# Two of four attention gate tiles computed as a seven-product pair in the last phase, not as filler in attention

## The chip, the core and the metric

The kernel runs on one core of a Trainium2 chip. The metric is the device time of one execution in microseconds; a kernel's time is the median of its timed runs. Beside them one execution was recorded by the hardware profiler, and every statement on what an engine did comes from that record.

## The reference

One layer of a decoder trunk, run in fp32 for 1024 prompt tokens and 64 sample tokens (8 sequences of 8) that share the weights. Cut to what matters here:

```
h = rmsnorm(x) * (1 + scale) + shift                  # width 1024
z = h @ w_in + b_in                                   # width 8456
a_u, a_v, a_g, b_q, b_k, b_v, b_g, c_qk, c_v, c_i, c_f, c_o, c_g, m_g = split(z)
ya = chunk_gmlp(a_u, a_v) * silu(a_g)
yb = sliding_window_attention(b_q, b_k, b_v) * silu(b_g)      # 8 heads of 64, window 128
yc = mlstm(c_qk, c_v, c_i, c_f, c_o) * silu(c_g)
merged = sum over the three branches of sigmoid(m_g[n]) * (y_n @ w_branch_n)
x_out = x + gate * (merged @ w_out)
```

The change concerns `b_g`, the 512 columns 2304 to 2816 of `w_in`: four channel tiles of 128, for all 1088 tokens, each put through `silu`.

## The kernel before

Every fp32 operand is split into a high and a low part (`hh`, `hl` for `h`), and a product is three matmuls: high by high, high by low, low by high. A channel tile against all tokens is worked in three chunks of 384, 384 and 320 tokens (`CH`), each of 8 k tiles x 3 matmuls.

The program runs in stages: the start, the mLSTM branch, the attention stage (pool `bph`), and the last phase. In the attention stage the order on TensorE is the order of the code (a manual schedule); the other engines' orders are set by the scheduler. A loop over steps `i` drives a pipeline of 16 prompt blocks (`Prompt(g, n)`: two key groups, eight blocks of 128 queries; here called blocks 0 to 15) and then 4 sample blocks. In step `i` the plan runs, in this order, `v` of block i-5 (the product with the values), `s` of block i-2 (the logits), `p` of block i-4 (the transposes of the probabilities), and `q` of block i (the transposes of the queries). After `s`, `p` and `q` a call of `filler` lets TensorE work on projections that attention does not wait for, so that VectorE and ScalarE have time for the softmax. A call ends at the first k tile at which the filled columns reach its share of `FILL`:

```
FILL = (11000, 11000)
PLAN = ((6, "y", 0), (5, "v", 0), (2, "s", 0.3), (4, "p", 0.3), (0, "q", 0.4))
order += [("a", s, n) for s in range(2) for n in range(9)]
order += [("b", f, ci) for f in range(4) for ci in range(3)][:-1]
```

The filler's order is: the query tiles (`q`, 256 columns for each 128 tokens), the gMLP rows (`a`, alike), and last the gates (`b`), tile `f` and chunk `ci`. A gate chunk's evacuation (`ev_b` in `bg_chunk`) is two ScalarE passes and one on VectorE, then a DMA from GpSimd's queue to the DRAM buffer `dsg`. The last chunk stays in PSUM across the end of the stage. Weights for the filler come in slabs of 256 columns, split by ScalarE and VectorE (L127, L128) into one of two `hl` buffers.

Between, VectorE also makes the sums `TT` of token halves and k halves for the last phase (`t_next`, L855 to L857 and L844).

A prompt block's softmax after the logits (L88 `pk<-KT,QT`): ScalarE copies and VectorE masks them (L1102, L1103), VectorE takes the maximum (L1106 to L1108, L1114), ScalarE the exponentials with their sums (L1111, L1115), VectorE adds the sink and takes the reciprocal (L1116, L1117), ScalarE scales (L1119); TensorE transposes (L92 `pu<-ident,Sm`); VectorE masks into `Pp` and `Pc` (L1131, L1134).

The last phase is a list `items` of TensorE pieces, each with weights prepared five items ahead (`LEAD`). Function `seven` forms two channel tiles as a pair: with channels, token halves and k halves as two by two blocks, seven products of 4 k tiles by 544 tokens replace eight. Each product is 4 x 3 matmuls on 288 tokens and as many on 256 (`CUT`); VectorE and ScalarE combine weights beforehand (`comb`, `w_split`, L1432, L1437, L1438) and results afterwards (`collect`), and `final` gets the four quarters. It is used for the gMLP's pairs and for the twelve pairs of merge gates (`gate_pair`). `gate_b(f, b)`, which stands behind the first branch's projections, multiplies a tile and token half of the attention result `dy` with the gates from `dsg`.

Of the kernel before, what the change touches and what calls it, by code (L numbers as in the profile page):

```python
# [11 lines left out]
AF = mybir.ActivationFunctionType  # L12
ALU = mybir.AluOpType
# [6 lines left out]
EPS = 1e-6  # L20
XP = 1115
XC = 1112
FILL = (11000, 11000)
PLAN = ((6, "y", 0), (5, "v", 0), (2, "s", 0.3), (4, "p", 0.3), (0, "q", 0.4))


# [3 lines left out]
CUT = ((0, 288), (288, 256))  # L30
# [11 lines left out]
def trunk_kernel(ctx: ExitStack, tc: tile.TileContext, I, O):  # L42
    nc = tc.nc
    V, S, G, T = nc.vector, nc.scalar, nc.gpsimd, nc.tensor

    w_in = I["w_in"][0]
# [30 lines left out]
    def slot(tag, shape, dt=F32, name=None):  # L77
        return sp.tile(shape, dt, tag=tag, name=name or tag)

    def ct(shape, name, dt=F32):  # L80
        return cp.tile(shape, dt, name=name)
# [13 lines left out]
    def kv(ap):  # L95
        return ap.rearrange("(k p) c -> p k c", p=128)

    def full(w, c0, n):
        v = kv(w[:, c0:c0 + n])
        return [v[:, 0:4], v[:, 4:8]]  # L100

    def pair(c0, c1):
# [3 lines left out]
    specs += [pair(2816 + 128 * h, 3328 + 128 * h) for h in range(1, 4)]  # L106
    specs += [pair(4360 + 128 * h, 4872 + 128 * h) for h in range(4)]
    specs += [full(w_in, 2048, 256), full(w_in, 1536, 256), full(w_in, 1792, 256),
              full(w_in, 512, 256), full(w_in, 768, 256), full(w_in, 2304, 256), full(w_in, 2560, 256)]

    slabs = {}

# [35 lines left out]
    cols = ct([128, 100], "cols")  # L148
    cwcol = ct([128, 32], "cwcol")
    bh = ct([128, 100], "bh")  # L150
    CAU, CAG, CBG, CQK, CO, CG, CM, CADA, CNG, CCB, CHN, CVN = 0, 4, 8, 12, 20, 24, 28, 52, 76, 84, 92, 96
# [323 lines left out]
    dsg = dp.tile([4, 128, NT], F32, name="dsg")  # L475
# [4 lines left out]
    with tc.tile_pool(name="cph", bufs=1, side="right", reuse_waits="tile") as c1:  # L480
# [303 lines left out]
        for h in range(1, 4):  # L784
            hl = next_slab()
            for s in range(2):
                f = 4 * s + h
# [89 lines left out]
    with tc.tile_pool(name="bph", bufs=1, side="right", reuse_waits="tile") as b1:  # L877
# [485 lines left out]
        def fill_steps():  # L1363
            order = [("q", 0, n) for n in range(9)]
            order += [("q", 1, n) for n in range(9)]
            order += [("a", s, n) for s in range(2) for n in range(9)]
            order += [("b", f, ci) for f in range(4) for ci in range(3)][:-1]
            for kind, a, c in order:
                yield from {"q": q_tile, "b": bg_chunk, "a": av_tile}[kind](a, c)
                done.add((kind, a, c))  # L1370

        fill = fill_steps()

        def filler(cols, until=None):
# [11 lines left out]
        for i in range(len(steps) + 6):  # L1386
            w = FILL[0] if i < 18 else FILL[1]
            for d, ph, share in PLAN:
# [15 lines left out]
    one.close()  # L1404


    w2r, w3, e2, w2 = (ctx.enter_context(tc.tile_pool(name=n, bufs=1, reuse_waits="tile")) for n in ("w2r", "w3", "e2", "w2"))
    banks = [0]

    def bank():  # L1410
# [3 lines left out]
    def part_(h, j):  # L1414
        return slice(HT * h + CUT[j][0], HT * h + CUT[j][0] + CUT[j][1])
# [4 lines left out]
    def mp(n, name):  # L1420
        return e2.tile([128, CUT[0][1]], F32, tag="mp", bufs=3, name=name)[:, :n]
# [39 lines left out]
    items = []  # L1461
# [134 lines left out]
    Q7 = (1, 6, 7, 5, 3, 2, 4)  # L1596
# [71 lines left out]
    def y_load(n):  # L1668
# [5 lines left out]
        for b in range(2):  # L1674
            c = slice(HT * b, HT * b + HT)
            for f in range(4):
# [2 lines left out]
                S.copy(yh[f][:, c], x)  # L1679
                V.tensor_tensor(yl[f][:, c], x, yh[f][:, c].bitcast(F32), ALU.subtract)  # L1680

    mh, ml = [None] * 8, [None] * 8
    lastm = [None] * 3

# [43 lines left out]
    def gate_rows(g):  # L1728
        def prep():
            for q in range(4):  # L1730
                if q % 2 == 0:
                    gst["t"] = gst.get("t", []) + [y2[0].tile([128, 2, 512], F32, tag=f"yh{2 + q // 2}", name="graw")]
                raw = gst["t"][-1][:, q % 2]
                with tc.issue_after(newest[0]):
                    nc.sync.dma_start(raw.rearrange("p (k c) -> p k c", k=2),
                                      kv(ada_w[:, 2048 + 256 * g:2304 + 256 * g])[:, 2 * q:2 * q + 2])
                gst[g, q] = raw

        def run(_):
            pm = gst[g] = bank()  # L1740
            for q in range(4):
                for kk in range(2):
                    i = 2 * (q % 2) + kk
                    mm(pm[32 * i:32 * i + 32, 0:256], sT[:, 2 * q + kk], gst[g, q][:, 256 * kk:256 * kk + 256], q < 2, q >= 2)
            gst[g, "s"] = mp(256, "gsb")
            S.copy(gst[g, "s"], pm[:, 0:256])
            gst[g, "m"] = mp(256, "mrow")[:9]
            nc.sync.dma_start(gst[g, "m"], ada_b[:, 2048 + 256 * g:2304 + 256 * g].broadcast_to([9, 256]))

        def run2(_):  # L1750
            pm, m = gst[g], gst[g, "m"]
            mm(pm[0:9, 256:512], sel, gst[g, "s"], True, True)
            V.tensor_tensor(m, m, pm[:9, 256:512], ALU.add)
            V.tensor_scalar(m, m, 0.5, None, ALU.mult)
            nc.sync.dma_start(drow[:, 256 * g:256 * g + 256], m)

        return [(prep, run), (None, run2)]
# [16 lines left out]
    gr = [x for g in range(4) for x in gate_rows(g)]  # L1774
    items += [(None, last_gate)] + it[0][:2] + [behind(t_late, 0, 1)] + it[0][2:4] + [behind(t_late, 2, 2), act(t_in_place, *((k,) for k in range(4)))] + it[0][4:5] + [act(t_late, (3,))] + it[0][5:]
    rest = it[1][:2] + [None] + it[1][2:3] + [None] + it[1][3:4] + [None] + it[1][4:5] + [None] + it[2][:1] + [None]
    rest += it[1][5:6] + [None] + it[1][6:] + [None] + it[2][1:2] + [None] + it[2][2:] + it[3]
    items += [x or gr.pop(0) for x in rest]

    def gate_b(f, b):  # L1780
        if not stage:
# [40 lines left out]
    for i, f in enumerate((0, 4, 1, 5, 2, 6)):  # L1822
        m_tiles(f)
        x = slot(("y0", "y1", "m2", "m3", "y4", "y5")[i], [128, NT], name="mgr")
# [19 lines left out]
    for i in range(4):  # L1844
# [4 lines left out]
        for n in tuple(range(9)) if i < 3 else (8,) + tuple(range(8)):  # L1849
# [15 lines left out]
            if n == 8:  # L1865
                t = mp(256, "ts")
# [39 lines left out]
```

## Time and profile before

| | |
|---|---|
| timed runs | 1182.39, 1181.17, 1179.51 us; median 1181.17 us |
| profiled execution | 1181.08 us, of which the core's span is 1179.4 us |
| mean granted TensorE clock | 0.996 |
| attention's prompt logits, first to last start | 404.3 to 526.9 us |
| gate finals in attention, first to last start (L1234) | 515.8 to 573.4 us |
| last phase, first product to the end of the span | 587.0 to 1179.4 us |

In the profile PE is TensorE, PEld its weight loads, DVE VectorE, ACT ScalarE, POOL GpSimd, SP the engine that issues most DMAs. A matmul's end in the record is modelled, and matmuls overlap in it; the distance from start to start tells its cost. A record of VectorE or ScalarE likewise reaches a little into the next one.

### The profile page before, as it was taken

The numbers are of one execution on the slowest core, as the hardware profiler recorded it, in microseconds if no ns is written. First come the engines' busy times: TensorE is split into PE (matmuls) and PEld (weight loads), VectorE is DVE, ScalarE is ACT, GpSimd is POOL, SyncE is SP. The second block draws the span as 40 slices with busy tenths as digits, with TensorE's granted clock in tenths as the row PEclk, the third lists the DMA queues.
The fourth block names the chain that finished last, engine by engine and source line by source line (L and its number), as shares of the span: only waits on it lengthen the run. The fifth ranks groups of instructions, "written<-read, shape, count | busy, mean of one in ns | idle before, by whom it ended". The sixth has DMA issues, their size and how long they took to land.

```text
span 1179.4 us, 23145 instructions
## 1 busy us (share of the span) xinstructions
PE 1154.0 (98%) x8924; PEld 1108.9 (94%) x8924; DVE 787.7 (67%) x1865; ACT 488.1 (41%) x1230; POOL 75.6 (6%) x109
## 2 busy tenths in 40 slices
PE   5999999999999999999999999999999999999998
PEld 3799999999999998988998999999999999999998
DVE  5678777655568577886699865555766676667433
ACT  4443455443333368877443443223332343235100
POOL 2000011111024010021000000000000000000000
PEclk8999999999999999999999999999999999999999
DMA  9821222223323111123135125545643353465422
GB/s 293 257 82 46 76 76 74 92 76 94 97 67 86 52 37 33 50 73 116 45 103 153 44 85 151 149 141 151 177 121 109 110 164 111 131 219 168 130 90 75
DMA packets 150773, 129.74 MB, mean 110 GB/s; under 512 B 13613, under 2 KB 140213, under 8 KB 150648
## 3 DMA queue, kind: packets, MB, share of 16 engines
q1 hardware_dynamic: 142984, 118.96, 34.3%
q0 software_dynamic: 2240, 7.08, 1.7%
q10 hardware_dynamic: 5440, 2.23, 0.7%
q8 instruction: 70, 1.15, 0.4%
q14 instruction: 39, 0.32, 0.1%
HBM read 99.39 MB, written 29.82 MB: 110 GB/s over the span
## 4 chain that ended last, share of the span: by engine, by line
PE 81%; DVE 9%; DMA 4%; ACT 3%; issue 2%; POOL 0%; SPq 0%; ACTq 0%; DVEq 0%; POOLq 0%
PE pg L88 42%; PE pk L88 24%; PE pu L88 13%; PE pk L92 2%; DMA stage<-dy 1%; DVE hl L128 1%; ACT Sm L1111 1%; DMA E<-scr 1%; DVE acc L498 1%; PE pu L92 1%; DMA xt<-in_x_prompt_dram 1%; DMA raw<-in_w_in_dram 1%; DVE vv L539 0%; DVE Sm L1103 0%; DMA fbb<-in_mlstm_f_bias_dram 0%
## 5 line engine op out<-in xcount | busy, mean ns | idle before, releaser
L88 PE MATMUL pg<-hl,hl 128*128 128x256 f32 (+3 forms) x904 | 277.3, 307 | 0.4 <-DVE hl L413 0.3
L88 PE MATMUL pg<-hh,hl 128*128 128x384 f32 (+1 forms) x912 | 236.9, 334 | 1.2 <-DVE hh L412 1.2
L88 PE MATMUL pg<-hl,hh 128*128 128x256 f32 (+1 forms) x1008 | 177.3, 283 | 0.0
L88 PEld LDWEIGHTS pg<-hl,hl 128*128 128x128 f32 x904 | 170.5, 189 | 2.0 <-DVE hl L413 1.2
L88 PEld LDWEIGHTS pg<-hh,hl 128*128 128x128 f32 x912 | 161.7, 189 | 4.4 <-issue 1.9
L88 PEld LDWEIGHTS pg<-hl,hh 128*128 128x128 f32 x1008 | 150.4, 188 | 0.3
L1437 ACT CAST prod<-raw 128x512 fp32r<-128x512 f32 x76 | 46.8, 620 | 130.1 <-PE pk L88 61.9
L88 PE MATMUL pg<-hh,prod 128*128 128x288 f32 (+1 forms) x400 | 83.9, 289 | 0.2 <-DVE prod L1438 0.2
L88 PE MATMUL pk<-hh,prod 128*128 128x256 f32 (+1 forms) x384 | 78.0, 285 | 0.0
L1438 DVE TENSOR_TENSOR prod<-raw,prod 128x512 fp32r<-128x512 f32 x76 | 51.9, 686 | 24.5 <-ACT prod L1437 24.3
L88 PEld LDWEIGHTS pg<-hh,prod 128*128 128x128 f32 x400 | 65.8, 188 | 1.1 <-DVE comb L1432 0.4
L1437 ACT CAST prod<-comb 128x512 fp32r<-128x512 f32 x60 | 37.0, 616 | 68.5 <-PE pk L88 26.3
L1601 ACT ACTIVATE tt<-tt,bh 128x288 f32<-128x288 f32 x96 | 49.9, 521 | 36.3 <-DVE tt L1563 14.2
L88 PEld LDWEIGHTS pk<-hh,prod 128*128 128x128 f32 x384 | 62.6, 188 | 0.8 <-DVE hl L844 0.4
L88 PE MATMUL pg<-yh,prod 128*128 128x288 f32 (+1 forms) x288 | 61.2, 290 | 0.0
L88 PE MATMUL pk<-yh,prod 128*128 128x256 f32 (+1 forms) x288 | 58.7, 285 | 0.0
L88 PE MATMUL pg<-hl,prod 128*128 128x288 f32 (+1 forms) x200 | 57.7, 289 | 0.0
L88 PE MATMUL pk<-tc,prod 128*128 128x256 f32 (+1 forms) x408 | 56.3, 287 | 0.0
L88 PE MATMUL pu<-hh,prod 128*128 128x288 f32 (+1 forms) x272 | 56.3, 287 | 0.0
L88 PE MATMUL pg<-tc,prod 128*128 128x288 f32 (+1 forms) x396 | 55.8, 290 | 0.0
L88 PE MATMUL pk<-hl,prod 128*128 128x256 f32 (+1 forms) x192 | 54.6, 284 | 0.0
L88 PEld LDWEIGHTS pk<-tc,prod 128*128 128x128 f32 x408 | 52.7, 188 | 1.3 <-issue 1.3
(551 smaller groups left out, 2642.5 us busy)
## 6 DMA issues: line engine op xcount, KB each, us to landing
raw<-in_w_in_dram SPq DMA_DIRECT2D x124, 256.0 KB
adaraw<-in_ada_w_dram SPq DMA_DIRECT2D x16, 512.0 KB
stage<-dy SPq DMA_DIRECT2D x24, 272.0 KB
dmg<-tt SPq DMA_DIRECT2D x44, 144.0 KB
dmg<-tt SPq DMA_DIRECT2D x44, 128.0 KB
mprev<-dmg SPq DMA_DIRECT2D x32, 144.0 KB
xt<-in_x_prompt_dram SPq DMA_DIRECT2D x8, 512.0 KB
graw<-in_ada_w_dram SPq DMA_DIRECT2D x16, 256.0 KB
```

Source lines behind the costliest of these rows:

```text
L88: T.matmul(out, lhsT=lhsT, rhs=rhs, start=start, stop=stop)
L92: T.transpose(out, in_, ident[:k, :k])
L128: V.tensor_tensor(hl[:, 1, off:off + m], raw[:, :m], hl[:, 0, off:off + m].bitcast(F32), ALU.subtract)
L498: V.scalar_tensor_tensor(acc, xp[:, j:j + XC], cwcol[:, 8 * j + f:8 * j + f + 1], acc, ALU.mult, ALU.add)
L1111: newS[0] = S.activation(Sm[:, h], Sm[:, h], AF.Exp, bias=nm[:, h:h + 1], scale=rr[:, h:h + 1], accum_out=dn[:, h:h + 1]).ins
L1437: a = S.copy(t[:, 0], x)
L1438: b = V.tensor_tensor(t[:, 1], x, t[:, 0].bitcast(F32), ALU.subtract)
L1601: S.activation(x, x, AF.Tanh, bias=bh[:, b:b + 1], scale=0.5)
```

## The change

Gate tiles 0 and 1 leave the filler, with their slab; each filler call's share shrinks with `FILL`; and the pair is formed by `seven` behind the gMLP's pairs, ahead of the first pair of merge gates. Its `final` is a new function that writes `dsg` from SP's queue. Tiles 2 and 3 stay in the filler. The order in which the last phase's SBUF pools are laid out changes too; they lie where the slabs and temporaries of the attention stage were.

```
-FILL = (11000, 11000)
+FILL = (9200, 9200)
...
-              full(w_in, 512, 256), full(w_in, 768, 256), full(w_in, 2304, 256), full(w_in, 2560, 256)]
+              full(w_in, 512, 256), full(w_in, 768, 256), full(w_in, 2560, 256)]
...
-            order += [("b", f, ci) for f in range(4) for ci in range(3)][:-1]
+            order += [("b", f, ci) for f in (2, 3) for ci in range(3)][:-1]
...
-    w2r, w3, e2, w2 = (ctx.enter_context(tc.tile_pool(...)) for n in ("w2r", "w3", "e2", "w2"))
+    e2, w3, w2r, w2 = (ctx.enter_context(tc.tile_pool(...)) for n in ("e2", "w3", "w2r", "w2"))
...
+    def bg_final(i, h, j, x):
+        t = mp(CUT[j][1], "tb")
+        S.activation(t, x, AF.Tanh, bias=bh[:, CBG + i:CBG + i + 1], scale=0.5)
+        S.activation(x, x, AF.Identity, bias=cols[:, CBG + i:CBG + i + 1], scale=1.0)
+        V.scalar_tensor_tensor(x, t, 1.0, x, ALU.add, ALU.mult)
+        nc.sync.dma_start(dsg[i, :, part_(h, j)], x)
...
-    items += [x or gr.pop(0) for x in rest]
+    items += [x or gr.pop(0) for x in rest] + seven((2304, 2432), Q7, bg_final)
```

What this does to the orders is shown at three places. First TensorE in step 4 of the attention loop, from the logits of block 2 to the transposes of block 0; `hh_...` and `hl_...` are k tiles of `h`, `hl` alone the weights. Before:

```order
L88 MATMUL pk<-KT,QT 128x256 x8
L88 MATMUL pg<-hl,hh_411 128x256 x2
L88 MATMUL pg<-hl,hl_412 128x256
L88 MATMUL pg<-hl,hh_501 128x256 x2
L88 MATMUL pg<-hl,hl_502 128x256
L88 MATMUL pg<-hl,hh_510 128x256 x2
L88 MATMUL pg<-hl,hl_511 128x256
L88 MATMUL pg<-hl,hh_601 128x256 x2
L88 MATMUL pg<-hl,hl_602 128x256
L88 MATMUL pg<-hl,hh_607 128x256 x2
L88 MATMUL pg<-hl,hl_608 128x256
L92 MATMUL pu<-ident,Sm 128x128 x4
```

The same place now:

```order
L88 MATMUL pk<-KT,QT 128x256 x8
L88 MATMUL pg<-hl,hh_607 128x256 x2
L88 MATMUL pg<-hl,hl_608 128x256
L88 MATMUL pg<-hl,hh_697 128x256 x2
L88 MATMUL pg<-hl,hl_698 128x256
L88 MATMUL pg<-hl,hh_703 128x256 x2
L88 MATMUL pg<-hl,hl_704 128x256
L88 MATMUL pg<-hl,hh_405 128x256 x2
L88 MATMUL pg<-hl,hl_406 128x256
L92 MATMUL pu<-ident,Sm 128x128 x4
```

Four k tiles of filler stand where five stood, and they come from an earlier place of the filler's order.

Second VectorE ahead of the reciprocal of block 15 (`es`; `dn` are the sums of its exponentials; `Sx`, `nms`, `dns` belong to sample blocks, `zb` is a gate chunk, `va` the gMLP rows' square sums). Before:

```order
L1183 TENSOR_REDUCE nms<-Sx 128x1
L1114 TENSOR_TENSOR es<-snk,nm 128x4
L1170 COPY kTs<-pk 128x512
L1165 TENSOR_TENSOR kcd<-kc,qgb 128x4x64 x2
L1184 SCALAR_TENSOR_TENSOR nms<-nms,nscol 128x1
L1235 SCALAR_TENSOR_TENSOR zb<-tb,zb 128x384
L1116 TENSOR_TENSOR es<-es,dn 128x4
L1189 TENSOR_TENSOR dns<-dns,ess 128x1
L1117 RECIPROCAL es<-es 128x4
```

Now:

```order
L1259 TENSOR_TENSOR vn<-ts,avb 64x128 x2
L1184 SCALAR_TENSOR_TENSOR nms<-nms,nscol 128x1
L1180 TENSOR_TENSOR Sx<-pk,smask 128x128
L1181 TENSOR_TENSOR Sx<-pk,smask 128x64
L1114 TENSOR_TENSOR es<-snk,nm 128x4
L1183 TENSOR_REDUCE nms<-Sx 128x1
L1235 SCALAR_TENSOR_TENSOR zb<-tb,zb 128x384
L1305 TENSOR_REDUCE vr<-va 128x9
L1116 TENSOR_TENSOR es<-es,dn 128x4
L1117 RECIPROCAL es<-es 128x4
```

The last gMLP row tile (`vn`) and its statistics, which lay well ahead of this place, now stand in it, and the sample blocks' logits have moved ahead of the reciprocal.

Third SP's queue in the last phase, around the first load of `dsg` for `gate_b(0, 0)` (`raw2_...` are weights of the last phase, `tt_...` result tiles). Before:

```order
L1427 DMA raw2_8541<-in_w_in_dram 128x4x128
L1785 DMA stage_8654<-dy_824 128x544
L1786 DMA stage_8654<-dsg_825 128x544
L1427 DMA raw2_8543<-in_w_in_dram 128x4x128
L1427 DMA raw2_8545<-in_w_in_dram 128x4x128
```

Now:

```order
L1427 DMA raw2_8621<-in_w_in_dram 128x4x128
L1688 DMA dsg_825<-tt_8265 128x288
L1688 DMA dsg_825<-tt_8286 128x256
L1688 DMA dsg_825<-tt_8187 128x288
L1688 DMA dsg_825<-tt_8202 128x256
L1688 DMA dsg_825<-tt_8154 128x288
L1688 DMA dsg_825<-tt_8169 128x256
L1688 DMA dsg_825<-tt_8228 128x288
L1794 DMA stage_8734<-dsg_825 128x544
L1427 DMA raw2_8623<-in_w_in_dram 128x4x128
L1688 DMA dsg_825<-tt_8243 128x256
```

Seven of the eight new writes stand between the first and the second weight load of the second gate pair, ahead of the load that reads them back.

More of the change, by code (lines that the diff above doesn't have):

```diff
@@ L1404, in trunk_kernel @@
     one.close()
-    w2r, w3, e2, w2 = (ctx.enter_context(tc.tile_pool(name=n, bufs=1, reuse_waits="tile")) for n in ("w2r", "w3", "e2", "w2"))
+    e2, w3, w2r, w2 = (ctx.enter_context(tc.tile_pool(name=n, bufs=1, reuse_waits="tile")) for n in ("e2", "w3", "w2r", "w2"))
     banks = [0]
```

## The prediction

> **What bounds the kernel now.** I read the page first, then the busy times by stage, then TensorE's waits, then the order of time on TensorE and VectorE in the attention stage. The page's head, its row of engines and its clock:
>
> ```profile
> span 1179.4 us, 23145 instructions
> PE 1154.0 (98%) x8924; PEld 1108.9 (94%) x8924; DVE 787.7 (67%) x1865; ACT 488.1 (41%) x1230; POOL 75.6 (6%) x109
> PEclk8999999999999999999999999999999999999999
> ```
>
> TensorE works through nearly the whole span, at full clock after the first slice. By stage (columns: window, length, then busy time and count of TensorE, its weight loads, VectorE, ScalarE, GpSimd; then clock and DMA):
>
> ```profile
> 404.00:468.00 64.00, 63.29 (x530) 59.06 (x529) 48.46 (x149) 45.34 (x175) 8.06 (x7) 1.00 0.17 48
> 468.00:526.00 58.00, 57.26 (x446) 51.98 (x446) 49.05 (x137) 47.51 (x180) 8.98 (x8) 1.00 0.21 60
> 526.00:587.00 61.00, 61.00 (x452) 55.40 (x452) 38.03 (x111) 34.53 (x111) 5.48 (x10) 1.00 0.28 79
> ...
> 685.00:1085.00 400.00, 399.64 (x3205) 399.19 (x3204) 259.00 (x524) 139.47 (x267) 0.00 (x0) 1.00 0.48 141
> ```
>
> The first two windows hold the sixteen prompt blocks of attention (0 to 15), eight in each; the third their end and the sample blocks; the last the gate pairs. TensorE bounds all four, but in the second VectorE is at 49.05 of 58.00 us: that is the stage from which filler is taken. TensorE's waits from 330 to 600 us, and its only one from 600 us on (waited for: total, times, longest):
>
> ```profile
> PE pk L92 <- DVE KT L1017: 1.2, 1, 1.2
> PE pk L92 <- DVE Sm L1103: 0.7, 1, 0.7
> PE pk L88 <- DVE QT L1071: 0.7, 1, 0.7
> PE pg L88 <- DVE prod L1438: 0.2, 1, 0.2
> ...
> PE pg L88 <- DVE yl L1680: 0.4, 1, 0.4
> ```
>
> So two of the three large waits are for attention's own VectorE work, and are short only because filler covers the rest. The fourth, 0.2 us, is the entry into the last phase.
>
> **The products: what TensorE saves.** Removed are 2 tiles x 8 k x 3 = 48 matmuls for each of the widths 384, 384 and 320; added are 7 products x 4 k x 3 = 84 for each of 288 and 256. Start to start, first and last of 18 matmuls of 384, three of 320, and nine each of 256 and 288 in the last phase:
>
> ```profile
> 561.14 0.33 PE L88 MATMUL pg<-hl,hl 128*128 128x384 f32 x1
> ...
> 564.26 0.34 PE L88 MATMUL pg<-hl,hl 128*128 128x384 f32 x1
> ...
> 521.44 0.31 PE L88 MATMUL pg<-hl,hl 128*128 128x320 f32 x1
> ...
> 521.88 0.31 PE L88 MATMUL pg<-hl,hl 128*128 128x320 f32 x1
> ...
> 772.64 0.28 PE L88 MATMUL pg<-yl,prod 128*128 128x256 f32 x1
> ...
> 773.69 0.28 PE L88 MATMUL pg<-yl,prod 128*128 128x256 f32 x1
> 774.06 0.29 PE L88 MATMUL pk<-yl,prod 128*128 128x288 f32 x1
> ...
> 775.25 0.30 PE L88 MATMUL pk<-yl,prod 128*128 128x288 f32 x1
> ```
>
> That is 173, 147, 117 and 132 ns. Removed: 96 x 0.173 + 48 x 0.147 = 23.7 us. Added: 84 x (0.117 + 0.132) = 20.9 us; the last window's mean, 400 / 3205 = 0.125 us, gives 168 x 0.125 = 21.0. TensorE saves 2.7 us of work.
>
> The Trainium skill, page "TensorE: Matmul & The Clock Gate", section "Back-to-back issue gap", speaks against this: in a stream of weight load and matmul it puts about 81 ns on 128 columns and 131 ns on 512, a large price for each matmul and a small one for each column. By that line (an estimate: 114, 106, 102 and 98 ns) 16.1 us would go and 16.8 come, and the trade would cost 0.7 us. The trace does not agree: from 256 to 384 columns it pays 56 ns, almost all of it by the column.
>
> **What lies beside TensorE in the last phase.** VectorE's means there (a final's SCALAR_TENSOR_TENSOR is priced by the last row's neighbours):
>
> ```profile
> L1438 DVE TENSOR_TENSOR prod<-raw,prod 128x512 fp32r<-128x512 f32 x62 | 42.5, 686 | 22.4 <-ACT prod L1437 22.4
> L1432 DVE TENSOR_TENSOR comb<-raw,raw 128x512 f32<-128x512 f32 x22 | 15.1, 688 | 9.7 <-DMA raw<-in_w_in_dram 9.7
> L1716 DVE SCALAR_TENSOR_TENSOR tt<-tt,pg 128x288 f32<-128x288 f32 x24 | 10.9, 453 | 10.1 <-PE pg L88 9.8
> ```
>
> Seven splits, four sums, fourteen collecting additions and eight finals make 7 x 0.69 + 4 x 0.69 + 22 x 0.44 = 17.3 us in the 21.0 us of the pair. It fits beside TensorE, whose eight PSUM banks are four products (12 us) ahead; ScalarE, at 139 of 400 us, has room too. The weight bytes are the same (1 MB). The eight writes of the gates move from GpSimd's queue to SP's, where seven stand between two weight loads; the next load there is for the gate pair after next. I take nothing for all this. If the cover fails, collecting waits for a tile not yet written out: at most the two microseconds that one product less of cover leaves, so 0 to 2. The new order of the SBUF pools puts the raw weights on the buffer of the gMLP rows' slab, which is read out before the gates' slab, so the first loads are free no later than now; the entry's 0.2 us wait stays.
>
> **The attention stage without the filler.** This decides. Here a block's logits must pass VectorE and ScalarE before TensorE transposes them two steps later. Block 8's logits and its reciprocal, block 15's logits, reciprocal and transposes; then the line of all reciprocals, and one scaling that follows a reciprocal:
>
> ```profile
> 467.83 1.22 PE L88 MATMUL pk<-KT,QT 128*128 128x256 f32 x8
> 480.62 0.17 DVE L1117 RECIPROCAL es<-es 128x4 f32<-128x4 f32 x1
> 525.92 1.22 PE L88 MATMUL pk<-KT,QT 128*128 128x256 f32 x8
> 541.79 0.17 DVE L1117 RECIPROCAL es<-es 128x4 f32<-128x4 f32 x1
> 545.12 0.75 PE L92 MATMUL pu<-ident,Sm 128*128 128x128 f32 x4
> ...
> 404.28 1.12 PE L88 MATMUL pk<-KT,QT 128*128 128x256 f32 x8
> ...
> L1117 DVE RECIPROCAL es<-es x16: 156/170/179, 413.3 to 541.8; 128x4 f32<-128x4 f32 x16
> ...
> 414.06 1.28 ACT L1119 ACTIVATE Sm<-Sm,es 128x128 f32<-128x128 f32 x4
> ```
>
> TensorE's side. Logits 8 to logits 15 take 58.1 us. Running the fill rule by hand, that stretch holds 79,424 filler columns before and 64,768 after; 14,656 fewer at 173 ns / 384 are 6.6 us, so 51.5 us are left. From logits 15 to the transposes it is 19.2 us now; 28,224 columns become 22,144, or 2.7 us less: 16.5.
>
> How long VectorE has between the two reciprocals without stopping TensorE: 51.5 + 16.5, less the shortest way from logits to reciprocal that the rows show (404.28 to 413.3, 9.0 us), less 1.5 us for the scaling and its signals: 57.5 us.
>
> VectorE's side. Means of the groups that carry its work in this stage:
>
> ```profile
> L1071 DVE TENSOR_TENSOR QT<-pk,QT 64x256 fp32r<-64x256 f32 x30 | 12.7, 422 | 4.8 <-ACT QT L1070 3.9
> L1103 DVE COPY_PREDICATED Sm<-mprv,pk 128x256 f32<-128x256 uint8 x28 | 11.2, 439 | 1.4 <-ACT Sm L1102 1.3
> L1134 DVE TENSOR_TENSOR Pc<-pu,mcT 128x512 f32<-128x512 f32 x16 | 10.9, 681 | 0.0
> L1106 DVE TENSOR_REDUCE nm<-Sm 128x4 f32<-128x512 f32 x16 | 10.8, 678 | 0.2
> L1259 DVE TENSOR_TENSOR vn<-pg,avb 128x128 f32<-128x128 f32 x32 | 8.9, 282 | 2.0 <-ACT pg L1261 1.0 <-PE pg L88 0.5
> L855 DVE TENSOR_TENSOR tx<-hh,tc 128x544 f32<-128x544 f32 x6 | 4.2, 719 | 1.6 <-PE pk L88 1.6
> L1116 DVE TENSOR_TENSOR es<-es,dn 128x4 f32<-128x4 f32 x16 | 2.6, 161 | 7.1 <-ACT es L1115 7.0
> ```
>
> Two rows that follow each other show how far records overlap:
>
> ```profile
> 488.29 0.71 DVE L857 TENSOR_TENSOR tx<-tx,hl 128x544 f32<-128x544 f32 x1
> 488.92 0.16 DVE L1117 RECIPROCAL es<-es 128x4 f32<-128x4 f32 x1
> ```
>
> The next starts 0.63 us after one of 0.71, so I take means some 0.07 us shorter (small ones a little less). In the changed order, what stands between those reciprocals: 14 masked copies at 0.37, 15 masked probabilities (L1131, L1134) at 0.60, 7 maxima at 0.66, 24 additions of the a tiles at 0.22, 12 lower halves of q (5.0 in all), 16 operations of the second sums for the products (L844, L855 to L857) at 0.65, 8 for q's norms (3.9), 4 weight splits (2.5), 9 for the samples' keys (3.9), 36 four-wide ones (5.2), and small rest 3.5: together 58.4 us. The same count over the order before gives 55.3 us: there 13 of the wide a-tile additions and five gate finals lie in the stretch, now 20 and one, because less filler a step leaves the a tiles for later.
>
> So 58.4 us of work meet a gap of 57.5: before, 55.3 met 58.1 + 19.2 - 12.8 - 1.5 = 63.0. TensorE must wait 0.9 us even if VectorE never idles. Before, the stretch took 61.2 us (480.62 to 541.79) for 55.3 of work, 5.9 of it idle, much of that for ScalarE, as the 7.0 us in the last row show. A busier VectorE idles less, but it also stands in order: the masked probabilities (L1131, L1134) wait for TensorE's transposes, and ahead of block 15's sum (L1116) stands a gate chunk's last pass (L1235), which waits for ScalarE. Idle time of 0 to 6.2 us makes the wait 0.9 to 7.1; I take half, 3.9, since neither end has a reason. Earlier blocks have some 2 to 5 us of room, where I take none. Behind the transposes everything on TensorE is in order, so such a wait is not regained; at the stage's end, after the 526 us row, VectorE has 38 of 61 us, and I take no more there.
>
> **The sum.** -2.7 + 3.9 = +1.2 us. The profiled execution lasted 1181.08 us around its span of 1179.4, and the median is 1181.17, so both give 1182.3.
>
> **The rivals.** (1) VectorE keeps up. For it: 5.9 idle microseconds were there to use, and TensorE had 0.7 us waits of its own to lose. The saving stays: 1181.1 - 2.7 = 1178.4, or 1179.3 with the 0.9. (2) VectorE falls behind in earnest: it idles as before, by a tenth, and each late block holds back the next block's logits through the three small banks. For it: two of the waits above are of this kind already. It decides from a wait of 5 us: with 7.1 us 1181.1 - 2.7 + 7.1 = 1185.5, with another 1.5 in the early blocks 1187. The Trainium skill, page "TensorE: Matmul & The Clock Gate", section "What's actually happening", says that an idle window of some 3.4 us halves the clock; no wait in the rows here is that long, no run here shows it, and only a single stop of that length would add to this rival. (3) The seven products save nothing, because each matmul pays mostly for being one: priced by rows as 168 at the 288 column's own 132 ns, they take 22.2 us, save 1.5, and give 1183.5. Against it stand the 117 and 132 ns side by side. By the line of the Trainium skill above it would be 1185.7. (4) The late writes delay the first gate pair: 2 us on top, 1184.3; against it the single 0.4 us wait after 600 us.
>
> **How the numbers follow.** The forecast (a stop of 1.5 to 5 us, 1179.9 to 1183.4) has 0.52, rival 1 0.19, rival 2 0.23, rivals 3 and 4 0.03 each. Three runs spread by 0.24%, so a change under 0.2% (2.4 us) can't be told from none. Faster by more needs nearly no stop, or a lost old wait besides: two thirds of rival 1, 0.13. Slower by more is rival 2, both small rivals and a part of the forecast's upper edge (0.08): 0.37. The same is the rest: 0.50. The range reaches from rival 1's full saving to rival 2: 1178.4 to 1186.5.
>
> **What would show it.** The products: about 168 matmuls of 256 and 288 columns more from 685 us on, all at 117 and 132 ns, and 144 fewer of 384 and 320 in attention. VectorE: over nine tenths busy between the reciprocals of blocks 8 and 15, TensorE's waits for Sm, QT or ScalarE's scaling grown to some 4 us in all, most of it from block 10 on. If these stay under 1 us, rival 1 was right; if TensorE waits in the early or the sample blocks, my choice of where the room ends was wrong; a wait beyond 685 us would be rival 4.

## The result and the profile after

The changed kernel takes 1191.58 us (median of 4 runs, 1188.96 to 1193.25) against 1180.95 us of the kernel before on the same chip (1179.51 to 1182.39): a ratio of 1.0090, interval 1.0077 to 1.0103. That is 10.6 us slower, where 1.2 us were predicted and the range ended at 1186.5.

The head of the page after, and the busy times by stage at the windows shown of before:

```profile
span 1191.5 us, 23220 instructions
PE 1157.8 (97%) x8948; PEld 1110.6 (93%) x8948; DVE 797.7 (67%) x1888; ACT 492.8 (41%) x1239; POOL 71.3 (6%) x103
...
404.00:468.00 64.00, 62.12 (x514) 57.20 (x514) 50.05 (x152) 47.51 (x174) 8.94 (x7) 1.00 0.19 51
468.00:526.00 58.00, 54.07 (x426) 47.71 (x422) 48.98 (x138) 44.38 (x176) 5.76 (x4) 0.97 0.14 38
526.00:587.00 61.00, 57.06 (x424) 51.26 (x423) 38.43 (x112) 33.84 (x112) 6.07 (x9) 0.97 0.33 95
...
685.00:1085.00 400.00, 399.60 (x3202) 399.36 (x3201) 258.15 (x521) 143.39 (x275) 0.00 (x0) 1.00 0.47 139
```

TensorE now stands idle for 4 us in each of the two windows that hold the late prompt blocks and the stage's end, and its clock, 1.00 in these windows before, is 0.97 in both. The last phase is as dense as it was.

TensorE's waits from 330 to 600 us after:

```profile
PE pu L92 <- ACT Sm L1119: 5.3, 2, 3.7
PE pk L92 <- DVE Sm L1103: 1.8, 1, 1.8
PE pk L88 <- DVE es L1114: 1.3, 1, 1.3
PE pk L92 <- DVE KT L1017: 1.2, 1, 1.2
PE pu L88 <- DVE Pc L1134: 0.6, 1, 0.6
PE pk L92 <- DVE QT L1071: 0.6, 1, 0.6
PE pg L88 <- DVE prod L1438: 0.2, 1, 0.2
```

They sum to 11.0 us; before it was 2.8, so TensorE waits 8.2 us more, all for the softmax of attention.

To split the difference, two marks in either kernel: the transposes of the keys (`kst`), which stand ahead of all attention blocks, and the first product of the last phase. The rows are a tile's instructions with their first and last start; first before, then after:

```profile
L92 PE MATMUL pk<-ident,kst x18: 223/272/302, 372.6 to 393.3; 128*128 128x128 f32 x16, 64*128 64x64 f32 x2
L88 PE MATMUL pg<-hh,prod x400: 276/293/400, 587.0 to 1062.1; 128*128 128x288 f32 x82, 128*128 128x256 f32 x52
```

```profile
L92 PE MATMUL pk<-ident,kst x18: 222/272/299, 374.7 to 395.3; 128*128 128x128 f32 x16, 64*128 64x64 f32 x2
L88 PE MATMUL pg<-hh,prod x432: 276/293/401, 578.9 to 1072.9; 128*128 128x288 f32 x89, 128*128 128x256 f32 x55
```

The start, where nothing was changed, took 2.1 us longer in this execution (the mark lay anywhere from 372.6 to 377.9 us in the profiles of this study). From the mark to the first product it is 214.4 us before and 204.2 after: 10.2 us won, where 23.7 us of products left. From there to the span's end it is 592.4 and 612.6: 20.2 us more, against 20.9 predicted. So 23.7 - 10.2 = 13.5 us were lost in the attention stage. 8.2 of them are the waits. The clock holds 3.4 more:

```profile
489.00:493.00 4.00, 4.00 (x21) 3.68 (x23) 3.37 (x13) 3.91 (x17) 0.00 (x0) 0.57 0.01 2
...
535.00:539.00 4.00, 0.48 (x3) 0.16 (x1) 1.41 (x7) 4.00 (x19) 1.65 (x3) 1.00 0.46 142
540.00:544.00 4.00, 4.00 (x16) 3.80 (x16) 1.29 (x2) 4.00 (x15) 0.01 (x1) 0.57 0.02 4
```

Behind a stop at 487 and another at 535 us, TensorE is busy all the time at a mean clock of 0.57 over 4 us: 4 x (1 - 0.57) = 1.7 us lost each time. The remaining 1.9 us are not idle time: between the marks TensorE stood idle for 2.7 us before and 10.8 after, so the listed waits hold all of that growth. In these 1.9 us the record has TensorE busy, and why stays open.

The last and longest stop, as VectorE and ScalarE lived it. Block 15's logits start at 518.87; its maximum, exponentials, reciprocal, scaling and transposes:

```profile
527.69 0.68 DVE L1106 TENSOR_REDUCE nm<-Sm 128x4 f32<-128x512 f32 x1
528.28 0.72 DVE L844 TENSOR_TENSOR tc<-tx,tc 128x544 fp32r<-128x544 f32 x1
...
530.44 0.71 DVE L844 TENSOR_TENSOR tc<-tx,tc 128x544 fp32r<-128x544 f32 x1
531.08 0.16 DVE L1107 TENSOR_TENSOR nm<-nm,r 128x4 f32<-128x4 f32 x1
...
533.21 0.15 DVE L1108 SCALAR_TENSOR_TENSOR nm<-nm,nsnk 128x4 f32<-128x4 f32 x1
...
538.05 0.18 DVE L1117 RECIPROCAL es<-es 128x4 f32<-128x4 f32 x1
...
538.78 1.27 ACT L1119 ACTIVATE Sm<-Sm,es 128x128 f32<-128x128 f32 x4
...
539.23 0.33 PE L92 MATMUL pu<-ident,Sm 128*128 128x128 f32 x1 [3.74 <-ACT Sm L1119]
```

The maximum is 8.8 us behind the logits (7.4 before), and the reciprocal 19.2 (15.9 before). The two tiny operations that follow the maximum (L1107, L1108) come 3.4 and 5.5 us after it: VectorE, without a gap from 524 to 534 us, works in between through second sums (L844), block 14's masked probabilities and the sample blocks' keys and logits. The wait is booked on ScalarE's scaling, but that could not start before VectorE had delivered the maximum.

### The profile page after: what moved, and what is told of

It reads as the page before. It is cut to its first block, busy times and chain, and to the rows that moved or that the text cites. A ratio compares the mean times of both kernels' runs of the same rounds, so it can differ in the third digit from the quotient of the medians.

```text
span 1191.5 us, 23220 instructions
## 1 busy us (share of the span) xinstructions
PE 1157.8 (97%) x8948; PEld 1110.6 (93%) x8948; DVE 797.7 (67%) x1888; ACT 492.8 (41%) x1239; POOL 71.3 (6%) x103
## 4 chain that ended last, share of the span: by engine, by line
PE 55%; DVE 2%; ACT 2%; DMA 2%; issue 0%; ACTq 0%; DVEq 0%; SPq 0%
PE pg L88 22%; PE pk L88 19%; PE pu L88 13%; DMA stage<-dy 1%; ACT Sm L1111 1%; PE pu L92 1%; DMA dy<-stage 0%; DMA raw<-in_w_in_dram 0%; PE pk L92 0%; DVE yl L1680 0%; DVE Sm L1103 0%; DVE prod L1438 0%; DVE Pc L1134 0%; DVE Pp L1131 0%; DVE hl L128 0%
## 5 line engine op out<-in xcount | busy, mean ns | idle before, releaser
L88 PE MATMUL pg<-hl,hl 128*128 128x256 f32 (+3 forms) x856 | 262.8, 307 | 0.4 <-DVE hl L413 0.3
L88 PE MATMUL pg<-hh,hl 128*128 128x384 f32 (+1 forms) x816 | 212.0, 336 | 1.2 <-DVE hh L412 1.2
L88 PEld LDWEIGHTS pg<-hl,hl 128*128 128x128 f32 x856 | 162.4, 190 | 2.4 <-DVE hl L413 1.6
L88 PEld LDWEIGHTS pg<-hh,hl 128*128 128x128 f32 x816 | 144.9, 189 | 4.3 <-issue 1.9
L88 PE MATMUL pg<-hh,prod 128*128 128x288 f32 (+1 forms) x432 | 90.7, 289 | 0.2 <-DVE prod L1438 0.2
L88 PE MATMUL pk<-hh,prod 128*128 128x256 f32 (+1 forms) x408 | 82.6, 284 | 0.0
L88 PEld LDWEIGHTS pg<-hh,prod 128*128 128x128 f32 x432 | 71.1, 188 | 1.1 <-DVE prod L1438 0.4
L88 PEld LDWEIGHTS pk<-hh,prod 128*128 128x128 f32 x408 | 66.4, 188 | 0.8 <-DVE tt L1555 0.4
L88 PE MATMUL pg<-hl,prod 128*128 128x288 f32 (+1 forms) x216 | 62.4, 289 | 0.0
L88 PE MATMUL pk<-tc,prod 128*128 128x256 f32 (+1 forms) x432 | 59.6, 287 | 0.0
```

The lines of the kernel that those rows point to most:

```text
L88: T.matmul(out, lhsT=lhsT, rhs=rhs, start=start, stop=stop)
```

## The experiments

The theory (V): TensorE's cover per block shrank below what VectorE needs for the same block, and VectorE, in order, delivers the softmax late; each long stop also costs a stretch at half clock (C). The rivals: ScalarE is the late engine (A), or the loss isn't in this stage or not from the cover (L). All comparisons are against the kernel before on the same chip, whose median was 1181.7 to 1181.9 us.

**The cover alone, without moving a product.**

```
-FILL = (11000, 11000)
+FILL = (9200, 9200)
```

> The kernel before with the filler's share cut from 11000 to 9200 and nothing moved; what the steps don't use is worked off at the end of the stage. Theory V: the waits of the changed kernel appear although no product was moved, some 7 to 8 us more waiting and 3.4 us of half clock: 1189 to 1193 us. If instead the loss came from the missing gate chunks, no change: 1181 us.

Measured: 1193.36 us, ratio 1.0102 (1.0086 to 1.0117). Its waits from 400 to 600 us, and the clock behind the longest:

```profile
PE pu L92 <- ACT Sm L1119: 6.8, 2, 5.3
PE pk L88 <- DVE es L1114: 1.3, 1, 1.3
...
537.00:541.00 4.00, 3.26 (x12) 2.94 (x13) 1.79 (x6) 4.00 (x15) 1.00 (x1) 0.57 0.02 4
```

The same stops, in the same places (420, 445, 486, 508 and 532 us, against 420, 446, 487, 512 and 535), with no gate chunk moved, and a loss of 11.5 us, just above the range that V gave. So the cover is the cause, and which products fill it is not. One half-clock stretch showed instead of two.

**The cover given back to the changed kernel** (`FILL` 11000).

> The changed kernel with the filler's share put back from 9200 to 11000. Theory V: in the prompt blocks TensorE's time per block is again that of the kernel before, the late waits go back to some 2 to 3 us and no half clock is seen before 530 us; the filler is used up about three steps earlier, and the sample blocks run bare: their own chains cost 3 to 8 us. Together 1181 to 1187 us. If the bare sample blocks cost as much as the cover that is gone (15 us), 1194 us. If the loss does not come from the share (a rearranged order alone), the waits stay: 1190 us.

Measured: 1191.48 us, ratio 1.0084 (1.0069 to 1.0098), no better than with 9200. The waits:

```profile
PE pu L92 <- ACT Sm L1119: 3.5, 1, 3.5
PE pu L92 <- ACT ys L1217: 3.0, 1, 3.0
PE pk L88 <- issue: 1.8, 1, 1.8
...
543.00:551.00 8.00, 5.51 (x28) 3.06 (x28) 2.78 (x12) 6.95 (x25) 0.55 (x1) 0.57 0.34 97
557.00:565.00 8.00, 4.95 (x32) 4.25 (x31) 4.54 (x16) 3.66 (x14) 0.57 (x1) 0.57 0.31 78
```

From 400 us up to block 15's logits no wait is over 0.5 us, better than V said; then the filler runs out early, and the end of the stage takes it all back, with two stretches at half clock of twice the length. The place of the loss was right and its size was not: I had allowed 3 to 8 us for bare sample blocks and nothing for the clock.

**Less work for VectorE: the second sums later.**

```
-        tail = {11: lambda: t_second(0), 13: lambda: t_second(1), 17: lambda: t_second(2),
-                18: seq(lambda: t_second(3), a_norm, lambda: a_scale(0)), 19: lambda: a_scale(1), ...
+        tail = {18: seq(a_norm, lambda: a_scale(0)), 19: seq(lambda: a_scale(1), lambda: t_second(0)),
+                20: seq(lambda: a_scale(2), a_load, lambda: t_second(1)), 21: seq(..., lambda: t_second(2), ...),
+                22: seq(lambda: t_second(3), ...
...
-            x = slot(("m1", "m1", "y2", "y3")[k], [128, HT], name="tx")
+            x = slot("m1", [128, HT], name="tx")
```

> The changed kernel, with the sixteen VectorE operations of the second sums (and their four ScalarE casts) moved from steps 11 to 18 of the attention loop to steps 19 to 22, behind the last prompt block's transposes. Theory V (VectorE's work per block is what TensorE waits for in blocks 8 to 15): 16 x 0.65 = 10.4 us leave the stretch, the four late waits (0.8, 2.0, 1.7 and 3.9 us) shrink to under 2 us in all, and the two stretches at half clock, which follow the two longest of them, go too: 1180 to 1184 us. Rival A (ScalarE is the late engine, since the two longest waits name its scaling): only 2.6 us of casts leave ScalarE, and 1187 to 1190 us remain. Rival L (the loss is the last phase's or the start's): no change, 1191 us.

> The kernel before, with the same move of the second sums. Theory V: there the waits are only some 2.6 us in all, so 1 to 2 us can be won: 1179 to 1181 us. Rival A: no change. If the later place is too late (VectorE is 89% busy from 587 to 685 us), both kernels get slower at the entry of the last phase, by up to 5 us.

Measured: 1189.75 us (ratio 1.0072, 1.0059 to 1.0084) for the changed kernel, 1191.77 us (1.0083, 1.0068 to 1.0097) for the kernel before. In the changed kernel every stop of blocks 8 to 15 is gone, and block 15's transposes start at 528.5 instead of 539.2 us; from the keys' transposes to the first product of the last phase it takes 196.6 us instead of 204.2. But that product now waits, and behind it the last phase takes 5.1 us longer (617.7 instead of 612.6); the row is the changed kernel's, and the kernel before has the same with 4.24:

```profile
570.29 0.61 PE L88 MATMUL pg<-hh,prod 128*128 128x288 f32 x1 [4.23 <-ACT prod L1437]
```

The sums, and with them the third sums and the first weights' split, reach the entry of the last phase late. So V is right on the stage, though not on the time, which by itself would fit A (1187 to 1190 us); and the place was wrong: the sums belong where they were. In the kernel before, where little was to be won, that alone costs 10 us, twice what was allowed for it.

**Only two sums later** (the third and fourth, to steps 19 and 20).

> The changed kernel with only the third and fourth of the second sums moved, from steps 17 and 18 to 19 and 20. Theory V: of the wait before block 15's transposes (3.9 us, 1.7 us of half clock behind it) most goes, the waits of blocks 5 to 12 stay, and half as many operations are pushed to the entry of the last phase as with all four: 1185 to 1189 us. If the entry takes all of it back: 1190 to 1192 us.

Measured: 1192.12 us, ratio 1.0089 (1.0076 to 1.0102). The scheduler put both sums where they had been: the orders of all engines are the changed kernel's. This is a repeat of the changed kernel and no test of V. It is of use below, for the clock.

**VectorE relieved in place: the sums on GpSimd.**

```
+        E = nc.gpsimd if q == 6 else V
-        V.tensor_tensor(x, v(half(hh, kk, b)), v(TT[prev, k][0]), ALU.subtract)
+        E.tensor_tensor(x, v(half(hh, kk, b)), v(TT[prev, k][0]), ALU.subtract)
...
```

> The changed kernel with the sixteen VectorE operations of the second sums done on GpSimd at the same places of the program (a selection of 128 x 1024 takes it 1.1 us, a subtraction of 128 x 544 perhaps 0.6 to 2.3 us; it is busy 15 of the 122 us of this stretch). Theory V: 10.4 us leave VectorE and nothing comes later, so the late waits and their half clocks go as with the later sums (468 to 526 us lost 8.1 us instead of 13.0) without the new waits at the entry of the last phase: 1180 to 1184 us. If GpSimd is so slow that the sums end after 579 us, the entry waits for them: 1186 to 1192 us. If VectorE slows down while GpSimd works, no gain: 1190 us or more.

> The kernel before with the second sums on GpSimd. Theory V: only some 2 us of waiting is there to win: 1179 to 1182 us. Any result above 1184 us says that GpSimd's work harms others (VectorE, or a queue of its DMAs), and by how much.

Measured: 1185.12 us for the changed kernel (ratio 1.0034, 1.0022 to 1.0047), 1184.58 us for the kernel before (1.0023, 1.0015 to 1.0032). Both lie above V's ranges. The kernel before got 2.9 us slower, by which its expectation would have GpSimd's work harm others; its trace doesn't show where (between the marks and in the last phase it takes 214.6 and 592.8 us, against 214.4 and 592.4), so that stays open. The changed kernel wins 6.5 us of its 10 back; one stop over 0.7 us is left, of block 6's logits at 444 us, with a half clock behind it. VectorE and GpSimd just ahead of it, the line of VectorE's additions (durations least, median, most), and the wait (with the sums on GpSimd, lines behind these stand two further down, so that L1116 is here the L1114 of before):

```profile
442.19 1.63 DVE L1033 TENSOR_TENSOR qraw<-ts,bqb 64x128 f32<-64x128 f32 x2
...
443.55 2.94 POOL L858 TENSOR_TENSOR tx<-tx,hl 128x544 f32<-128x544 f32 x1
...
L1033 DVE TENSOR_TENSOR qraw<-ts,bqb x4: 276/279/1428, 403.0 to 443.5; 64x128 f32<-64x128 f32 x4
...
PE pk L88 <- DVE es L1116: 3.2, 1, 3.2
```

Both engines are slow there: one of the two 64 x 128 additions took 1.43 us, where the median of the line is 0.28, and an addition of 128 x 544 on GpSimd 2.94, where the quickest on this line took 1.35. Hence the next kernel, which keeps that first sum on VectorE (`if q == 6 and k`):

> As the changed kernel with the sums on GpSimd, but the first of the four second sums stays on VectorE: with all four there, GpSimd's first sum ran at 440 to 447 us beside a burst of VectorE work that took longer there, and TensorE stopped for 3.2 us with 1.7 us of half clock behind it. Theory V with contention as its second half: that stop shrinks to the 1.3 us that the changed kernel had there, block 10's stop of 0.6 to 1.8 us may return, and no half clock is left: 1180 to 1183 us, the first version of the changed kernel that isn't slower than before. If the 3.2 us stop had another cause, it stays: 1185 us.

> The kernel before with three of the four second sums on GpSimd, the control to the changed kernel so treated (1181.8 us). Neither is held up much by VectorE, so the difference of the two is the worth of the move itself, 23.7 us of TensorE's work against 20.9. If that trade is what the prediction says, -2.7 us, this kernel stands at 1182 to 1185 us; if it is worth nothing, at 1180 to 1182 us, as the kernel before.

Measured: 1181.82 us for the changed kernel (ratio 1.0001, 0.9992 to 1.0010) and 1182.05 us for the kernel before (1.0004, 0.9994 to 1.0015). The stretch between the reciprocals of blocks 8 and 15, in the kernel before, in the changed one, and in the changed one with three sums on GpSimd:

```profile
480.62:541.79 61.17, 60.42 (x449) 54.49 (x450) 52.54 (x146) 47.72 (x177) 10.06 (x10) 1.00 0.17 50
```

```profile
472.33:538.05 65.72, 59.22 (x462) 51.71 (x460) 55.91 (x158) 48.60 (x190) 6.55 (x6) 0.97 0.16 44
```

```profile
471.26:527.72 56.46, 55.58 (x457) 49.74 (x455) 49.26 (x137) 46.43 (x184) 20.87 (x15) 1.00 0.15 43
```

With the cover of 9200 untouched, 6.7 us less of VectorE's work (55.91 to 49.26) shorten the stretch by 9.3 us, no half clock is seen, and the 10 us are gone. ScalarE's work changed little (48.60 to 46.43), so A falls. Between the two kernels so treated, each measured against the kernel before on its own chip, the move itself is worth 0.2 us by the medians, less than their intervals can tell from none; the trade of products alone was to give 2.7. The marks show where the rest went in the profiled executions: of the 23.7 us that left attention 21.3 arrive (213.3 to 192.0 us, with 1.9 us more idle time of TensorE), and the last phase grew by 20.4.

**More cover on top** (`FILL` 9800).

> The same with the filler's share at 9800 instead of 9200. Theory V: the stops that are left (early blocks, block 10) get shorter by up to 1 us each, and the filler ends about one sample step earlier, which costs 0 to 3 us: 1179 to 1184 us. If the end of the stage is as tight as with 11000 (stops of 9 us behind block 15), 1186 us or more.

Measured: 1185.06 us, ratio 1.0021 (1.0011 to 1.0031): 3 us worse with more cover, and above V's range. One stop of 4.5 us came up before block 10's transposes, with its half clock. In it:

```profile
490.89 1.00 DVE L1110 SCALAR_TENSOR_TENSOR nm<-nm,nsnk 128x4 f32<-128x4 f32 x1
...
493.55 1.21 DVE L1116 TENSOR_TENSOR es<-snk,nm 128x4 f32<-128x4 f32 x1
...
490.51 1.36 POOL L856 TENSOR_TENSOR tx<-hh,tc 128x544 f32<-128x544 f32 x1 [5.46 <-PE pg L88]
...
493.38 1.36 POOL L858 TENSOR_TENSOR tx<-tx,hl 128x544 f32<-128x544 f32 x1
```

Four-wide operations on the softmax's path, 0.16 us elsewhere, took 1.0 and 1.2 us while GpSimd worked; and ScalarE, in order, ran the next block's exponentials before the scaling that TensorE waited for. Both follow from the orders that the scheduler set at this share, which I did not foresee; how much each of the two cost isn't shown.

**The cover shifted from early to late steps** (`w = 8400 if i < 9 else 10400`).

> The changed kernel with the share 8400 in steps 0 to 8 and 10400 from step 9 on, about as many columns in all. Theory V, with room in the early blocks as the prediction had it (2 to 5 us): the late stops (1.8, 1.5 and 3.7 us) and their half clocks shrink to under 3 us in all, the early ones grow by at most 2: 1184 to 1188 us. If the early blocks have no room either, what is won late is lost early: 1190 to 1193 us.

Measured: 1194.13 us, ratio 1.0105 (1.0089 to 1.0120). The early stops are just as long as with 9200 (0.5 and 1.3 us), so the early blocks did have room; but the late ones only moved, to blocks 10 and 15 and a sample block (3.0, 1.7 and 2.4 us):

```profile
PE pu L92 <- ACT Sm L1119: 4.7, 2, 3.0
PE pu L88 <- DVE dns L1189: 2.4, 1, 2.4
```

Neither expectation holds: the time lies 1 us above the second's range, and its reason does not fit. The profiled execution, of 1190.0 us span, was also faster than the median.

**The clock by itself.** Twenty unused matmuls fill the wait before block 15's transposes.

```
+                if self.g == 1 and n == 7:
+                    for _ in range(20):
+                        mm(pT[:, 0:384], hh[0][:, 0:128], hh[1][:, 0:384], True, True)
```

> The changed kernel with twenty matmuls of 384 columns put before the transposes of block 15, into the bank that these overwrite; their result is not used. They take 20 x 0.173 = 3.5 us and lie in the wait of 3.9 us. Theory C (a stop of TensorE is followed by a stretch at half clock, a cost apart from the wait itself): the transposes start when they did, the granted clock stays 1.00 from 539 to 543 us, and 1.7 us are won: 1189 to 1191 us against 1191.6. Rival (the half clock has another cause, or is only how the record shows slow matmuls): the clock row is unchanged, 1191.5 to 1192 us.

Measured: 1187.70 us, ratio 1.0049 (1.0037 to 1.0061), 3.9 us below the changed kernel's median and 1.3 below the range expected. The fill, the transposes, and the stage by the granted clock:

```profile
533.53 3.65 PE L88 MATMUL pu<-hh,hh 128*128 128x384 f32 x20
537.44 0.33 PE L92 MATMUL pu<-ident,Sm 128*128 128x128 f32 x1 [0.26 <-ACT Sm L1119]
...
526.00:587.00 61.00, 60.55 (x453) 55.07 (x452) 39.66 (x112) 32.81 (x107) 6.07 (x9) 1.00 0.36 103
```

From block 15's logits to its transposes it took 20.4 us, as without the fill, so nothing in the softmax got faster; from the transposes to the first product it took 38.1 us instead of 39.7, and the clock stayed at 1.00. Those 1.6 us are the clock's price. The rest of the 3.9 us isn't explained by the edit: in this execution the stop at 487 us was 1.0 us long and cost no clock.

## Why the prediction was wrong

Right were the price of the added products and the last phase: 20.2 us came there, against 20.9 predicted, and beyond 600 us there is the single wait of 0.4 us of before, so writes, weights and pools cost nothing (rivals 3 and 4 fall). Right was the place of the loss, VectorE's order between the reciprocals of blocks 8 and 15, and the growth of its work there (3.1 us by the orders; 52.54 to 55.91 measured). The sum failed in three terms.

1. *The wait in the late blocks, "0.9 to 7.1; I take half".* From block 8's logits (461.31 after) to block 15's transposes it took 77.3 us before and 77.9 after, although 9.1 us of filler had gone (20,224 columns in the traces; the count by hand, of 79,424 and 64,768 columns up to block 15's logits where the traces hold 81,984 and 67,840, gave 9.3). So 9.7 us were lost, where 3.9 were predicted: 7.0 more in the listed waits, 1.7 of clock, and 1.0 in which TensorE is recorded busy.

   The step that failed is "a busier VectorE idles less". By the windows above, VectorE idled 9.8 of 65.7 us, where it had idled 8.6 of 61.2. The prediction had that as 5.9 and allowed 0 to 6.2, because its count of VectorE's work was too high: 55.3 where the window holds 52.5, and 58.4 where it holds 55.9. In its own terms: 11.0 us from block 8's logits to its reciprocal (9.0 taken), 55.9 of work (58.4), 9.8 idle (3.0), and 1.2 to the transposes (1.5) make the 77.9. VectorE was busy for 85% of the stretch, not for over nine tenths. Less cover did not press its idle time out. In the last stop, for one, it stood idle for 1.4 us ahead of the gate chunk's last pass (L1235) and for 0.9 ahead of the sum (L1116), both for ScalarE; how all of its idle time divides wasn't measured.

2. *"Earlier blocks have some 2 to 5 us of room, where I take none."* From block 0's logits to block 8's it got 6.4 us shorter (63.5 to 57.2), where 18,176 fewer filler columns at 173 ns / 384 are 8.2: 1.8 us lost, 1.3 of them in one stop at 446 us, which the uneven share left as it was.

3. *The clock, at nothing.* I had put the price of a stop to the clock only on a single wait of 3.4 us, which no row of before showed, and gave it no term. Two stretches at half clock cost 3.4 us, 1.7 of them in the first term's stretch; that one followed a stop of 1.80 us only. Where a sum forecasts new stops, their clock price belongs in the sum.

Of the late blocks 9.7 - 3.9 = 5.8 us, of the early ones 1.8, and the second half-clock stretch's 1.7 make 9.3; over the predicted 1182.3 that gives 1191.6, and 1191.58 was measured. That it fits so closely is luck: the executions differ by more. Rival 2 (VectorE falls behind in earnest, 1185.5 to 1187) had the right way; it too stopped at the upper end of the same bound, took the idle time before as 5.9 and left out the clock.

What stays open: the stops can't be worked out from a block's cover and VectorE's sum alone. With shares of 9200, 9800, 10400 and 11000 they stood at other blocks each time, and the scheduler's orders on VectorE and ScalarE differed each time; the 9800 were measured with sums on GpSimd, the 10400 in the late steps alone. No version measured here beats the kernel before; the best of the changed ones equals it.

## What to carry to other kernels

Filler on the bounding engine is not spare work: before it is moved elsewhere, compare per block the time that the engine behind it needs including its present idle time, read from a window of the profile, not its busy time alone. Give a forecast stop of TensorE of two microseconds or more a clock term: here most such stops cost 1.7 us on top, some 3.4, one nothing. If the work must move, relieve the lagging engine in place first, and look at where the scheduler then puts the operations on the path.

## What the runs showed of the hardware

The half clock comes in pieces of fixed length: between 330 and 1170 us the traces hold twelve stretches, nine of 3.41 us (a mean of 0.57 over 4 us) and three of 6.83 (0.57 over 8 us). Within a trace they lie on one grid of 3.413 us: in the changed kernel stretches start at 24.91, 38.56, 489.12 and 540.32 us, which is 4, 132 and 15 such lengths apart. The Trainium skill, page "TensorE: Matmul & The Clock Gate", section "What's actually happening", tells of a free-running activity window of about 3.4 us; the length and the grid agree. Its idle condition, a window of that length, is stricter than what was seen. Cut along each trace's grid, a window at full clock in which TensorE stood idle for 0.56 or more was followed by half clock in all nine cases, one of 0.45 or less in none; of six between 0.47 and 0.54 three were. So it matters how a stop lies on the grid. The same stop of 1.80 us, at the same place of the same order, halved the clock in the changed kernel, where one window held all of it, and not in its repeat (a_two_late), where the grid cut it in two; of either, the row of the stop, then that window (TensorE busy for 1.60 and 1.99 of 3.41 us) and the next:

```profile
488.90 0.53 PE L92 MATMUL pk<-ident,qraw 128*128 128x128 f32 x2 [1.80 <-DVE Sm L1103]
485.71:489.12 3.41, 1.60 (x15) 1.40 (x14) 3.38 (x10) 1.94 (x9) 0.00 (x0) 1.00 0.71 195
489.12:492.53 3.41, 3.41 (x17) 3.21 (x15) 2.84 (x8) 3.36 (x16) 0.00 (x0) 0.50 0.01 2
```

```profile
489.76 0.44 PE L92 MATMUL pk<-ident,qraw 128*128 128x128 f32 x2 [1.80 <-DVE Sm L1103]
485.97:489.38 3.41, 1.99 (x18) 1.79 (x16) 3.41 (x10) 2.20 (x10) 0.00 (x0) 1.00 0.70 191
489.38:492.79 3.41, 3.03 (x25) 2.46 (x25) 3.09 (x9) 3.36 (x14) 0.00 (x0) 1.00 0.02 6
```

The uneven share's stop of 3.02 us was cut likewise, into windows idle for 0.48 and 0.40, and cost no clock.

GpSimd and VectorE hold each other up: the 1.0, 1.2 and 1.4 us for operations of 0.16 to 0.28 us all stood beside GpSimd's sums. In the five kernels with sums on GpSimd, 37 operations of VectorE between 400 and 600 us took 0.3 us or more above the median of their kind; every one lay beside such a sum, and the 22 smallest of them, of one to four columns, ended 0.01 to 0.02 us after a GpSimd operation ended. The two rows at 490.89 and 493.55 us above show it: they end at 491.89 and 494.76, GpSimd's at 491.87 and 494.74. Other operations beside GpSimd's sums were not held up so long. The Trainium skill, page "GPSIMD Engine Reference", section "1. Specifications", names this for VectorE's instructions with two SBUF inputs, which these are.
